# Seven block products instead of eight for one token group's MLP up projection, and a new order of the two groups

## The chip, the core and the metric

The kernel runs on one core of a Trainium2 chip. The metric is device time in microseconds (us) of one launch, as the median of several runs. A core has five engines that run side by side and wait for each other through semaphores: TensorE (PE in the profile; PEld is its weight load), VectorE (DVE), ScalarE (ACT), GpSimd (POOL) and SyncE (SP), which here issues most of the transfers. Matmuls write PSUM, eight banks of 128 x 512 floats; everything else lives in SBUF.

## The reference

The program is one layer of a hybrid decoder over 1024 prompt tokens and 64 sampled tokens (8 sequences of 8), with a model width of 1024. The part that the change touches is the end of the layer:

```python
x = x + mixed @ lw['w_out']
h2 = rmsnorm(x, lw['g_mlp'])
x = x + jnp.square(jax.nn.relu(h2 @ lw['w_up'])) @ lw['w_down']
gate = jax.nn.sigmoid(rmsnorm(x, lw['g_ple']) @ lw['w_ple_gate'])
x = x + gate * (p @ lw['w_ple_proj'])
```

w_up is 1024 x 4096, w_down 4096 x 1024; all data are 32-bit floats. Ahead of this stand the input projection, the three mixers (a recurrent one, a short convolution, and attention, for the sampled tokens over a paged cache) that produce `mixed`.

## The kernel before

**Precision.** A float operand is split in two parts of the type fp32r: a rounded high part (ScalarE copies it to that type) and the remainder (VectorE or GpSimd subtracts). A product of two split operands is three matmuls, high x high, high x low, low x high, accumulated in PSUM (`gemm_t`, L162). Weights are loaded in 512 KB pieces into a raw buffer "wr" (two of them), ScalarE casts them and GpSimd, or VectorE for w_down, subtracts (`Weights.load`, L147). The split weights have two buffers for each part.

**Token groups.** The 1088 tokens are held transposed (model dimension on partitions). Group A is tokens 0 to 511, in one chunk of 512 columns; group B is the other 576 (512 prompt and 64 sampled) in two chunks of 288. `Part` (L1157) holds a group's residual x, its operands h (tag "big"), its activations (tag "act", four buffers) and scratch (tag "tmp").

**The MLP.** It goes in 16 blocks of 256 columns of w_up. `up(parts, fb)` (L1252) multiplies a block's weights with h, and takes max(., 0) times the norm's factor rb, squares it (rb is a token's 1/rms, so h itself doesn't wait for it), and splits the result into ah and al. `down(parts, fb, acts)` (L1269) multiplies these with the matching rows of w_down and adds the result to x, 128 rows and one chunk at a time. `mlp` (L1283) issues the up of block n+1 ahead of the down of block n. PSUM results of both go round three banks (`acc`).

**Order.** The code is written in an order of priority. A scheduler at build time plays it through and lets each engine take the first instruction that is ready, so work written later fills gaps ahead of it; the order on each engine is then fixed. Buffers of a pool go round, and a new pool placed over a released one waits for the tiles that it covers. Group A's output projection, norm and first 14 blocks are written behind attention and decode, and fill TensorE there. `out_proj(B)` can only start when decode is done. The calls in question:

```python
    out_proj(A, 4, 4)
    A.norm("g_mlp", acc, wide=True)
    mlp(*(([A], fb) for fb in range(NA - 1)))
    out_proj(B)
    B.norm("g_mlp", banks(6, 7))
    mlp(([A], NA - 1), *(([B], fb) for fb in range(NA)), *(([A, B], fb) for fb in range(NA, 16)))
```

With NA = 15, block 14 of A follows B's output projection, then come B's blocks 0 to 14, and block 15 for both groups together, whose weights are loaded once. Last come the norms for both groups (`Part.norm`, L1199), the gate and the output (`ple`, L1340). `norm` writes x times the gain, split, as h, and forms rb from the squares: sums on VectorE and GpSimd, a matmul against ones, a root, a reciprocal, and a matmul that spreads it.

Of the kernel before, what the change touches and what calls it, by code (L numbers as in the profile page):

```python
# [41 lines left out]
NA = 15  # L42
# [6 lines left out]
def hybrid_step(ctx: ExitStack, tc: tile.TileContext, I, O):  # L49
# [6 lines left out]
    def f(t):  # L56
        return t.bitcast(F32)
# [958 lines left out]
    W = Weights(wpool)  # L1016
    mpa = tc.alloc_tile_pool(name="mlp_a", bufs=1, reuse_waits="tile")
# [139 lines left out]
    class Part:  # L1157


        def __init__(self, pool, t0, n, chunks):  # L1160
            self.pool, self.t0, self.n, self.chunks = pool, t0, n, chunks
            self.x = pool.tile([128, 8, n], F32, name="x")
            self.tiles = range(t0 // 128, -(-(t0 + n) // 128))

        def big(self, name):
            return [[self.pool.tile([128, 4, self.n], F32R, name=f"{name}{e}{g}", tag="big", bufs=4) for g in range(2)]
                    for e in "hl"]
# [31 lines left out]
        def norm(self, gain, bank, wide=False):  # L1199

            self.h = self.big("n")
            for m in range(8):
                hi, lo = (self.h[e][m // 4][:, m % 4, :] for e in range(2))
                S.activation(hi, self.x[:, m], AF.Copy, scale=P1(gain, m))
                V.scalar_tensor_tensor(lo, self.x[:, m], P1(gain, m), f(hi), op0=ALU.mult, op1=ALU.subtract)  # L1205
            sums, sq = self.act("sums", F32), [self.act("sq", F32) for _ in range(2)]
# [31 lines left out]

    w_up, w_down = I["w_up"][0], I["w_down"][0]

    def out_proj(p, k0=0, nk=8, bank=acc):
        nm = 16 // nk
        x = [h[k0 // 4:] for h in p.h]
        for m0 in range(0, 8, nm):
            w = W.load(w_out[k0 * 128:(k0 + nk) * 128, m0 * 128:(m0 + nm) * 128], nk=nk, ncol=nm * 128)
            for m in range(m0, m0 + nm):
                for t0, n in p.chunks:
                    ps = bank()
                    gemm_t(ps, w, m - m0, x, t0, n, nk=nk)
                    V.tensor_add(p.x[:, m, t0:t0 + n], ps[:, :n], p.x[:, m, t0:t0 + n])  # L1250

    def up(parts, fb):  # L1252
        w = W.load(w_up[:, fb * 256:fb * 256 + 256])
        acts = []
        for p in parts:
            ah, al = p.act("ah", F32R), p.act("al", F32R)
            acts.append((ah, al))
            for m in range(2):
                for t0, n in p.chunks:
                    ps = acc()  # L1260
                    gemm_t(ps, w, m, p.h, t0, n)
                    r = p.tmp("r")
                    V.scalar_tensor_tensor(r[:, :n], ps[:, :n], 0.0, p.rb[:, t0:t0 + n], op0=ALU.max, op1=ALU.mult)  # L1263
                    S.square(r[:, :n], r[:, :n])
                    S.copy(ah[:, m, t0:t0 + n], r[:, :n])
                    V.tensor_sub(al[:, m, t0:t0 + n], r[:, :n], f(ah[:, m, t0:t0 + n]))
        return parts, fb, acts

    def down(parts, fb, acts):  # L1269
        wh, wl = W.load(w_down[fb * 256:fb * 256 + 256, :], nk=2, ncol=1024, sub=V)  # L1270
        for p, (ah, al) in zip(parts, acts):
            for m in range(8):
                c = slice(m * 128, m * 128 + 128)
                for t0, n in p.chunks:
                    ps = acc()
                    for k in range(2):
                        a, b = ah[:, k, t0:t0 + n], al[:, k, t0:t0 + n]
                        PE.matmul(ps[:, :n], wh[:, k, c], a, start=k == 0, stop=False)  # L1278
                        PE.matmul(ps[:, :n], wh[:, k, c], b, start=False, stop=False)  # L1279
                        PE.matmul(ps[:, :n], wl[:, k, c], a, start=False, stop=k == 1)  # L1280
                    V.tensor_add(p.x[:, m, t0:t0 + n], ps[:, :n], p.x[:, m, t0:t0 + n])  # L1281

    def mlp(*blocks):  # L1283

        before = None
        for parts, fb in blocks:
            u = up(parts, fb)
            if before:
                down(*before)
            before = u  # L1290
        down(*before)
# [3 lines left out]
    A = Part(mpa, 0, 512, ((0, 512),))  # L1295
# [15 lines left out]
    B = Part(mpb, 512, 576, ((0, 288), (288, 288)))  # L1311
# [53 lines left out]
    for p in (A, B):  # L1365
        p.norm("g_ple", banks(3, 4))
        ple_inputs(p)
    for sl in range(4):
        w = W.load(wg_[:, sl * 256:sl * 256 + 256])
        w2_ = W.load(wp_[:, sl * 256:sl * 256 + 256], nk=2, tag="wp")  # L1370
# [4 lines left out]
    mpa.release()  # L1375
# [28 lines left out]
```

## Time and profile before

| | us |
|---|---|
| median of 3 runs | 1771.43 |
| lowest, highest | 1764.46, 1772.76 |
| the profiled execution, its own time | 1768.19 |
| span in its profile | 1766.5 |
| TensorE busy | 1700.9 (96%) |
| VectorE busy | 1013.9 (57%) |
| ScalarE busy | 702.3 (40%) |
| GpSimd busy | 484.9 (27%) |

The span is from the first to the last instruction of the profiled execution; the 1.7 us beside it lie outside of the span. A matmul's duration in the profile covers its way through the array, and the next one starts earlier, so the number of matmuls in a stretch tells more than their durations. In rows of the timeline the columns are start, duration, engine, line, operation, output and inputs with their shapes; a bracket gives idle time ahead and what ended it. Rows of groups have a count, the busy time and the mean duration in ns.

### The profile page before, as it was taken

How to read it: one execution, taken by the hardware profiler on the slowest of the kernel's cores; microseconds unless marked ns; L12 is line 12 of the kernel's file. 1: busy time of each engine (PE TensorE's matmuls, PEld its weight loads, DVE VectorE, ACT ScalarE, POOL GpSimd, SP SyncE). 2: the span in 40 equal slices, each digit the busy share in tenths (PEclk: the TensorE clock that was granted, in tenths of full speed). 3: DMA queues.
4: the chain of work that ended last, by engine and by line, in shares of the span. 5: the costliest groups of instructions: out<-in, count | busy, mean ns of one | idle time of the engine just before them, and what ended most of it. 6: DMA issues, size and time to landing. Idle time of an engine off the chain costs nothing.

```text
span 1766.5 us, 29840 instructions
## 1 busy us (share of the span) xinstructions
PE 1700.9 (96%) x11933; PEld 1522.0 (86%) x11933; DVE 1013.9 (57%) x1634; ACT 702.3 (40%) x1283; POOL 484.9 (27%) x412
## 2 busy tenths in 40 slices
PE   6999899999999899999998999999999999999998
PEld 5898888888988777888876666999999999998898
DVE  6266954554576689778754334345555555548432
ACT  6633323323453567555533332442232223235321
POOL 4123322312300353232335452332221221113310
PEclk9999999999999899999999999999999999999999
DMA  5134356434523553333245453532222222221221
GB/s 183 50 115 136 106 151 178 117 92 118 139 77 110 188 173 95 128 124 112 85 122 166 140 161 106 176 94 90 79 76 92 76 92 72 96 75 53 67 63 40
DMA packets 195149, 194.87 MB, mean 110 GB/s; under 512 B 57729, under 2 KB 166945, under 8 KB 194882
## 3 DMA queue, kind: packets, MB, share of 16 engines
q1 hardware_dynamic: 189890, 176.18, 33.3%
q0 software_dynamic: 5120, 16.78, 3.2%
q8 instruction: 94, 1.54, 0.4%
q14 instruction: 45, 0.37, 0.1%
HBM read 155.92 MB, written 36.98 MB: 109 GB/s over the span
## 4 chain that ended last, share of the span: by engine, by line
PE 56%; DVE 3%; DMA 2%; POOL 1%; issue 1%; ACT 0%; SPq 0%; ACTq 0%; POOLq 0%; DVEq 0%
PE b L170 10%; PE b L171 10%; PE b L169 10%; PE b L1278 6%; PE b L1279 6%; PE b L1280 6%; PE b L910 1%; DVE nl L1205 1%; PE b L1145 1%; PE b L1120 1%; PE b L1115 1%; DMA kpg<-in_cache_k,idx 1%; PE b L921 1%; PE b L920 1%; DVE x L1281 1%
## 5 line engine op out<-in xcount | busy, mean ns | idle before, releaser
L159 POOL TENSOR_TENSOR wl<-wr,wh 128x1024 fp32r<-128x1024 f32 (+1 forms) x116 | 291.6, 2532 | 580.8 <-ACT wh L158 571.0
L169 PE MATMUL b<-nh,wh 128*128 128x288 f32 (+1 forms) x960 | 316.1, 330 | 2.2 <-DVE x L1250 2.2
L170 PE MATMUL b<-nl,wh 128*128 128x288 f32 (+1 forms) x960 | 315.9, 329 | 1.6 <-DVE nl L1205 1.6
L171 PE MATMUL b<-nh,wl 128*128 128x288 f32 (+1 forms) x960 | 315.2, 329 | 0.0
L158 ACT CAST wh<-wr 128x1024 fp32r<-128x1024 f32 (+1 forms) x178 | 177.7, 1041 | 277.9 <-PE b L1279 183.5
L1281 DVE TENSOR_TENSOR x<-b,x 128x288 f32<-128x288 f32 (+1 forms) x384 | 200.7, 532 | 130.9 <-PE b L1280 130.7
L1278 PE MATMUL b<-ah,wh 128*128 128x288 f32 (+1 forms) x768 | 256.9, 334 | 6.5 <-DVE x L1281 6.0
L1280 PE MATMUL b<-ah,wl 128*128 128x288 f32 (+1 forms) x768 | 251.9, 328 | 0.0
L1279 PE MATMUL b<-al,wh 128*128 128x288 f32 (+1 forms) x768 | 251.9, 328 | 0.0
L170 PEld LDWEIGHTS b<-nl,wh 128*128 128x128 f32 x960 | 180.5, 188 | 16.1 <-issue 2.7
L169 PEld LDWEIGHTS b<-nh,wh 128*128 128x128 f32 x960 | 180.3, 188 | 16.3 <-DVE x L1250 2.9
L171 PEld LDWEIGHTS b<-nh,wl 128*128 128x128 f32 x960 | 180.4, 188 | 12.7 <-issue 0.8
L1278 PEld LDWEIGHTS b<-ah,wh 128*128 128x128 f32 x768 | 144.6, 188 | 25.4 <-DVE x L1281 9.9
L1279 PEld LDWEIGHTS b<-al,wh 128*128 128x128 f32 x768 | 144.7, 188 | 10.4 <-issue 1.6
L1280 PEld LDWEIGHTS b<-ah,wl 128*128 128x128 f32 x768 | 144.5, 188 | 10.2
L790 PE MATMUL b<-wh,h_hi 128*128 128x256 f32 x432 | 129.4, 300 | 3.7 <-ACT nat L797 3.7
L791 PE MATMUL b<-wl,h_hi 128*128 128x256 f32 x432 | 127.1, 294 | 0.0
L792 PE MATMUL b<-wh,h_lo 128*128 128x256 f32 x432 | 127.0, 294 | 0.0
L1263 DVE SCALAR_TENSOR_TENSOR r<-b,rb 128x288 f32<-128x288 f32 (+1 forms) x96 | 51.0, 533 | 119.7 <-PE b L171 116.8
L169 PE MATMUL b<-h_hi,wh 128*128 128x384 f32 (+1 forms) x336 | 115.5, 344 | 1.4 <-ACT xs L330 1.3
L170 PE MATMUL b<-h_lo,wh 128*128 128x384 f32 (+1 forms) x336 | 113.4, 337 | 0.0
L171 PE MATMUL b<-h_hi,wl 128*128 128x384 f32 (+1 forms) x336 | 112.5, 335 | 0.0
(375 smaller groups left out, 3286.5 us busy)
## 6 DMA issues: line engine op xcount, KB each, us to landing
wr<-in_w_up SPq DMA_DIRECT2D x62, 512.0 KB
wr<-in_w_down SPq DMA_DIRECT2D x62, 512.0 KB
wr<-in_w_in SPq DMA_DIRECT2D x26, 512.0 KB
wr<-in_w_out SPq DMA_DIRECT2D x16, 512.0 KB
xt<-in_x_prompt SPq DMA_DIRECT2D x8, 512.0 KB
stk_s<-sth SPq DMA_DIRECT2D x32, 128.0 KB
stk_s<-stl SPq DMA_DIRECT2D x32, 128.0 KB
out<-nat SPq DMA_DIRECT2D x16, 256.0 KB
```

The source lines that it names most:

```text
L158: S.copy(wh[:, flat], raw[:, :n * ncol])
L159: (sub or G).tensor_sub(wl[:, flat], raw[:, :n * ncol], f(wh[:, flat]))
L169: PE.matmul(ps[:, :n], wh[:, k, c], a, start=(k == 0), stop=False)
L170: PE.matmul(ps[:, :n], wh[:, k, c], b, start=False, stop=False)
L171: PE.matmul(ps[:, :n], wl[:, k, c], a, start=False, stop=(k == nk - 1))
L790: PE.matmul(o, a, w[0][:, k, :], start=(k == 0), stop=False)
L791: PE.matmul(o, a, w[1][:, k, :], start=False, stop=False)
L792: PE.matmul(o, b, w[0][:, k, :], start=False, stop=(k == 7))
L1278: PE.matmul(ps[:, :n], wh[:, k, c], a, start=k == 0, stop=False)
L1279: PE.matmul(ps[:, :n], wh[:, k, c], b, start=False, stop=False)
L1280: PE.matmul(ps[:, :n], wl[:, k, c], a, start=False, stop=k == 1)
L1281: V.tensor_add(p.x[:, m, t0:t0 + n], ps[:, :n], p.x[:, m, t0:t0 + n])
```

## The change

**Seven products.** For group B, the up product of a block is seen as a 2 x 2 block product: the weights in four blocks a[m, k] (128 columns m, half k of the 1024 inputs), h in four blocks (half of the inputs, chunk of 288 tokens). Winograd's form of Strassen's scheme forms it from seven products of block sums instead of eight products of blocks. `up7` makes four sums of weight blocks on GpSimd (`s_`), splits seven weight operands (three into the common ring "w", four into buffers "ws"), runs seven products of four k each, and combines them with seven additions on VectorE, p1 being copied by ScalarE. `operands` makes B's seven split operands from x, the gain and rb: the sums are of normalized values, so rb has to be there first, and the evacuation no longer multiplies by it. The differences run on VectorE, the remainders on GpSimd for 11, 2, 3, 4 and on VectorE for 21, 1, 22. The products go round banks 0 to 3, the downs of B banks 4 to 7.

**Order.** A's block 14 up moves ahead of `out_proj(B)`; behind it come B's `rms` (the second half of `norm`) and its operands 11, 2, 3, 4, then A's up 15 and downs 14 and 15. Then A's h and work pools are released, B's operands 21, 1, 22 and the buffers of `up7` are placed over them, and B's 16 blocks run alone. A's norm for the gate is written ahead of B's last down.

**Weights in pieces.** `load` cuts a load into pieces of 128 x 512, high and low, in a ring of ten each, in place of whole loads in two buffers; the raw loads are the same 512 KB. All products read them through `gemm_p`. Block 15's weights are loaded for A and for B.

```diff
+    def split_piece(src, sub=None, pool=None, tag="w", bufs=10):
+        hl = [(pool or wpool).tile([128, 512], F32R, name=f"{tag}{e}", bufs=bufs) for e in "hl"]
+        h3, l3 = (t.rearrange("p (k c) -> p k c", k=src.shape[1]) for t in hl)
+        S.copy(h3, src)
+        (sub or G).tensor_sub(l3, src, f(h3))
+        return hl
...
+        def operands(self, gain, ids, pool, bufs):
...
+            for k in range(4):
+                h = self.act("hk", F32)
+                for e in range(2):
+                    V.scalar_tensor_tensor(h[:, e], self.x[:, 4 * e + k], P1(gain, 4 * e + k), self.rb, op0=ALU.mult,
+                                           op1=ALU.mult)
+                t = self.act("tk", F32)
+                val = {11: h[:, 0, :n], 21: h[:, 1, :n], 22: h[:, 1, n:], 1: t[:, 0, :n], 2: t[:, 0, n:],
+                       3: t[:, 1, :n], 4: t[:, 1, n:]}
+                if need & {1, 2, 4}:
+                    V.tensor_sub(val[1], h[:, 0, n:], val[11])
+                if need & {2, 4}:
+                    V.tensor_sub(val[2], val[22], val[1])
+                if 4 in need:
+                    V.tensor_sub(val[4], val[21], val[2])
+                if 3 in need:
+                    V.tensor_sub(val[3], val[22], h[:, 0, n:])
+                for i in ids:
+                    S.copy(out[i][:, 0, k], val[i])
+                    (V if i in (21, 1, 22) else G).tensor_sub(out[i][:, 1, k], val[i], f(out[i][:, 0, k]))
...
+    def up7(p, fb, ops, pool):
+        r = [raw_weights(w_up, 4 * k, 4, fb * 256, 256) for k in range(2)]
+        a = {(m, k): r[k][:, :, 128 * m:128 * m + 128] for m in range(2) for k in range(2)}
...
+        w = {11: split_piece(a[0, 0])}
+        G.tensor_add(s_[0], a[1, 0], a[1, 1])
+        G.tensor_sub(s_[1], s_[0], a[0, 0])
+        G.tensor_sub(s_[2], a[0, 0], a[1, 0])
+        w[12] = split_piece(a[0, 1])
+        G.tensor_sub(s_[3], a[0, 1], s_[1])
+        w[22] = split_piece(a[1, 1])
+        for i in (2, 1, 3, 4):
+            w[i] = split_piece(s_[i - 1], pool=pool, tag="ws", bufs=4)
...
+        def out(m, e, c):
+            t = slice(e * n, e * n + n)
+            V.scalar_tensor_tensor(c, c, 0.0, c, op0=ALU.max, op1=ALU.mult)
+            S.copy(ah[:, m, t], c)
+            G.tensor_sub(al[:, m, t], c, f(ah[:, m, t]))
...
+        p1 = pool.tile([128, n], F32, name="p1")
+        S.copy(p1, product(11, 11))
+        out(0, 0, add("c", product(12, 21), p1))
+        u2 = add("u2", product(2, 2), p1)
+        p5 = product(1, 1)
+        v = add("v", p5, u2)
+        u3 = add("u3", product(3, 3), u2)
+        out(1, 1, add("c", p5, u3))
+        out(0, 1, add("c", product(4, 22), v))
+        out(1, 0, add("c", product(22, 4), u3))
...
-    mlp(*(([A], fb) for fb in range(NA - 1)))
+    u = up(A, 0)
+    for fb in range(1, NA):
+        u, before = up(A, fb), u
+        down(*before)
     out_proj(B)
-    B.norm("g_mlp", banks(6, 7))
-    mlp(([A], NA - 1), *(([B], fb) for fb in range(NA)), *(([A, B], fb) for fb in range(NA, 16)))
+    B.rms(banks(6, 7))
+    ops = B.operands("g_mlp", (11, 2, 3, 4), mpb, 4)
+    for fb in range(NA, 16):
+        u, before = up(A, fb), u
+        if fb < 15:
+            down(*before)
+    down(*before)
+    down(*u)
+    wka.release()
+    hpa.release()
+    hpb = tc.alloc_tile_pool(name="h_b", bufs=1, reuse_waits="tile")
+    ops.update(B.operands("g_mlp", (21, 1, 22), hpb, 3))
+    up_bank, down_bank = banks(0, 1, 2, 3), banks(4, 5, 6, 7)
+    u = up7(B, 0, ops, hpb)
+    for fb in range(1, 16):
+        u, before = up7(B, fb, ops, hpb), u
+        down(*before, bank=down_bank)
...
-    for p in (A, B):
-        p.norm("g_ple", banks(3, 4))
-        ple_inputs(p)
+    A.norm("g_ple", banks(0, 1))
+    ple_inputs(A)
+    down(*u, bank=down_bank)
+    B.norm("g_ple", banks(3, 4))
+    ple_inputs(B)
```

More of the change, by code (lines that the diff above doesn't have):

```diff
@@ L1237, in norm @@
                     V.reciprocal(self.rb[:, t0:t0 + n], self.rb[:, t0:t0 + n])
+        def operands(self, gain, ids, pool, bufs):
+            n = self.n // 2
+            out = {}
+            for i in ids:
+                t = pool.tile([128, 4, 2 * n], F32R, name=f"op{i}", tag="big", bufs=bufs)
+                out[i] = t.rearrange("p k t -> p (k t)").rearrange("p (e k t) -> p e k t", e=2, k=4)
+            need = set(ids)
+            for k in range(4):
[14 more added lines that the diff above has]
+                    V.tensor_sub(val[3], val[22], h[:, 0, n:])
+                for i in ids:
+                    S.copy(out[i][:, 0, k], val[i])
+                    (V if i in (21, 1, 22) else G).tensor_sub(out[i][:, 1, k], val[i], f(out[i][:, 0, k]))
+            return out
     w_up, w_down = I["w_up"][0], I["w_down"][0]
@@ L1248, in out_proj @@
                     ps = bank()
-                    gemm_t(ps, w, m - m0, x, t0, n, nk=nk)
+                    gemm_p(ps, w, m - m0, x, t0, n, nk=nk)
                     V.tensor_add(p.x[:, m, t0:t0 + n], ps[:, :n], p.x[:, m, t0:t0 + n])
[L1252 to L1291, printed above, removed]
+    def up(p, fb):
+        w = load(w_up[:, fb * 256:fb * 256 + 256], 8, 256)
+        ah, al = p.act("ah", F32R), p.act("al", F32R)
+        for m in range(2):
+            for t0, n in p.chunks:
+                ps = acc()
+                gemm_p(ps, w, m, p.h, t0, n)
+                r = p.tmp("r")
+                V.scalar_tensor_tensor(r[:, :n], ps[:, :n], 0.0, p.rb[:, t0:t0 + n], op0=ALU.max, op1=ALU.mult)
+                S.square(r[:, :n], r[:, :n])
+                S.copy(ah[:, m, t0:t0 + n], r[:, :n])
+                V.tensor_sub(al[:, m, t0:t0 + n], r[:, :n], f(ah[:, m, t0:t0 + n]))
+        return p, fb, ah, al
@@ L1293, in hybrid_step, with down @@
+    def down(p, fb, ah, al, bank=acc):
+        w = load(w_down[fb * 256:fb * 256 + 256, :], 2, 1024, sub=V)
+        for m in range(8):
+            for t0, n in p.chunks:
+                ps = bank()
+                gemm_p(ps, w, m, ([ah], [al]), t0, n, nk=2)
+                V.tensor_add(p.x[:, m, t0:t0 + n], ps[:, :n], p.x[:, m, t0:t0 + n])
     w_out = I["w_out"][0]
-    A = Part(mpa, 0, 512, ((0, 512),))
+    A = Part(xpa, wka, hpa, 0, 512, ((0, 512),))
     A.load_x(acc)
@@ L1310, in hybrid_step @@
     mpb = tc.alloc_tile_pool(name="mlp_b", bufs=1, side="right", reuse_waits="tile")
-    B = Part(mpb, 512, 576, ((0, 288), (288, 288)))
+    B = Part(mpb, mpb, mpb, 512, 576, ((0, 288), (288, 288)))
     B.load_mix(range(8))
@@ L1374, in hybrid_step @@
     mpb.release()
-    mpa.release()
+    wka.release()
+    xpa.release()
     wpool.release()
```

75 lines of the change are left out of this document (64 added, 11 removed).

## The prediction, made before the change was run

> **What bounds the kernel now.** I read the page's engine totals and its forty slices first, then busy time by stage, then the groups of one steady stretch.
>
> ```profile
> span 1766.5 us, 29840 instructions
> PE 1700.9 (96%) x11933; PEld 1522.0 (86%) x11933; DVE 1013.9 (57%) x1634; ACT 702.3 (40%) x1283; POOL 484.9 (27%) x412
> PE   6999899999999899999998999999999999999998
> ```
>
> ```profile
> core 0: us, PE busy (x) PEld busy (x) DVE busy (x) ACT busy (x) POOL busy (x), PEclk, DMA share, GB/s
> 900.00:950.00 50.00, 43.18 (x247) 31.58 (x245) 23.41 (x45) 15.19 (x25) 30.29 (x27) 0.93 0.55 160
> ...
> 1300.00:1350.00 50.00, 50.00 (x379) 50.00 (x379) 26.48 (x52) 14.83 (x24) 9.04 (x5) 1.00 0.26 79
> ...
> 1600.00:1650.00 50.00, 46.16 (x272) 39.79 (x271) 40.85 (x61) 31.24 (x55) 23.40 (x12) 1.00 0.18 55
> ...
> 1700.00:1766.00 66.00, 61.10 (x388) 55.95 (x386) 19.42 (x37) 12.25 (x27) 3.67 (x2) 0.99 0.15 43
> ```
>
> TensorE is the bound: in 1300:1350 it has no gap, while VectorE (DVE) is busy 26.5 of 50 us, GpSimd (POOL) 9.0, and the DMA share is 0.26. So removing a matmul there removes time, as long as nothing else rises to 50. A matmul's listed duration isn't its price, since matmuls overlap: 379 in 50 us is **0.132 us each** at 288 columns. For 512 columns I count starts:
>
> ```profile
> 900.58 0.39 PE L171 MATMUL b<-nh,wl 128*128 128x512 f32 x1
> ...
> 903.30 0.39 PE L171 MATMUL b<-nh,wl 128*128 128x512 f32 x1
> ```
>
> Twelve matmuls in 2.72 us: **0.227 us each**. The steady groups between 1250 and 1550 us give the other prices (count, busy us, mean ns):
>
> ```profile
> L171 PE MATMUL b<-nh,wl 128*128 128x288 f32 x384 | 113.2, 295 | 0.0
> L1281 DVE TENSOR_TENSOR x<-b,x 128x288 f32<-128x288 f32 x186 | 84.0, 456 | 54.9 <-PE b L1280 54.9
> L159 POOL TENSOR_TENSOR wl<-wr,wh 128x1024 fp32r<-128x1024 f32 x23 | 57.3, 2513 | 245.7 <-ACT wh L158 245.7
> L158 ACT CAST wh<-wr 128x1024 fp32r<-128x1024 f32 x48 | 48.1, 1049 | 139.3 <-PE b L1279 118.7 <-PE b L170 20.5
> L159 DVE TENSOR_TENSOR wl<-wr,wh 128x1024 fp32r<-128x1024 f32 x24 | 28.3, 1222 | 5.9 <-ACT wh L158 5.9
> L1266 DVE TENSOR_TENSOR al<-r,ah 128x288 fp32r<-128x288 f32 x47 | 27.6, 587 | 35.2 <-ACT ah L1265 35.2
> L1265 ACT CAST ah<-r 128x288 fp32r<-128x288 f32 x47 | 20.4, 434 | 1.5
> ```
>
> **Part 1, the matmuls removed.** A block is 256 columns of w_up and the matching rows of w_down. For B a block's up product is now 2 row tiles x 2 token chunks x 8 k x 3 terms = 96 matmuls of 288 columns; seven products x 4 k x 3 terms are 84 of the same shape. Sixteen blocks: 192 fewer, x 0.132 = **-25.3 us**. A steady B block (up and down) falls from 192 matmuls, 25.3 us, to 180, 23.7 us.
>
> **Part 2, what the seven products ask of the other engines, per 23.7 us block.** GpSimd: seven weight splits and four sums or differences of 512 columns at half of 2.513 (1.26 us), four activation remainders of 288 columns at 0.72 (half of the 1.43 us quoted below for 576): 13.8 + 2.9 = 16.7 us, up from about 5. VectorE: 16 output adds and 7 product adds at 0.456, four squarings at 0.415, four splits of w_down at 0.61: 14.6 us. ScalarE: 11 casts at 0.52 and five copies at 0.434: 7.9 us. All lie beside 23.7 us of TensorE. The loads stay 2 MB a block; A's last block is no longer shared, so four 512 KB loads on SP's queue and their splits are added, at a DMA share of 0.26: 0 us, and some 5 us in all if the next weights were late, which the ring of ten pieces, seven a block, makes unlikely. If cover is thin it is at VectorE: an operation with two SBUF inputs can meet a GpSimd operation.
>
> ```profile
> 1599.95 4.78 POOL L159 TENSOR_TENSOR wl<-wr,wh 128x1024 fp32r<-128x1024 f32 x2 [45.06 <-ACT wh L158]
> ...
> 1602.33 2.95 DVE L1205 SCALAR_TENSOR_TENSOR nl<-x,par,nh 128x512 fp32r<-128x512 f32 x1
> ...
> 1605.80 0.74 DVE L1205 SCALAR_TENSOR_TENSOR nl<-x,par,nh 128x512 fp32r<-128x512 f32 x1
> ...
> PE b L1278 <- DVE x L1281: 3.3, 7, 1.5
> ...
> L1205 DVE SCALAR_TENSOR_TENSOR nl<-x,par,nh 128x576 fp32r<-128x576 f32 x16 | 15.7, 1005 | 2.4 <-ACT nh L1204 2.4
> ```
>
> The same instruction took 0.74 us with GpSimd idle and 2.95 us when GpSimd was in its second subtraction (1602.3 to 1604.7); operations whose other input is PSUM (456 ns throughout) show nothing of it. Eight of VectorE's 31 operations per new block are of the first kind; each may wait up to 1.26 us, and TensorE's evacuations queue behind it. Two runs of four PSUM banks allow about three groups (3 x 6 x 0.132 = 2.4 us) of delay. From the waits row, seven such stalls cost 3.3 us in the one stretch where VectorE was as mixed; I take 0.2 us a block, **+3 us**, ends 0 and 16 (1 us a block).
>
> The page "SBUF — State Buffer" of the Trainium skill, section "Who interferes with whom", says that a VectorE instruction with two SBUF inputs and a GpSimd instruction that reads SBUF exclude each other for a whole instruction. By that rule, the trace agrees (2.95 against 0.74 us).
>
> **Part 3, the gap before B's first new product.** This is the term I had to choose. B's operands can be formed only from the finished x and its norm, and B's first block needs all of op11 and op21. What covers this is A's block 15 up, and downs 14 and 15: 3 x 48 matmuls x 0.227 = 32.7 us after out_proj(B). Before, only rb was late, and it was needed only at an evacuation.
>
> ```profile
> 1167.99 0.29 PE L171 MATMUL b<-mh,wl 128*128 128x288 f32 x1
> 1168.12 0.39 PE L169 MATMUL b<-nh,wh 128*128 128x512 f32 x1
> ...
> 1168.86 0.45 DVE L1250 TENSOR_TENSOR x<-b,x 128x288 f32<-128x288 f32 x1
> 1169.23 3.73 DVE L1205 SCALAR_TENSOR_TENSOR nl<-x,par,nh 128x576 fp32r<-128x576 f32 x5
> ...
> 1180.21 1.17 PE L1220 MATMUL b<-onesq,sums 128*128 128x1 f32 x10
> ...
> 1187.46 0.70 ACT L1231 COPY rb<-b 128x512 f32<-128x512 f32 x2 [2.47 <-PE b L1229]
> ...
> 1189.73 0.83 DVE L1266 TENSOR_TENSOR al<-r,ah 128x288 fp32r<-128x288 f32 x2 [0.83 <-ACT ah L1265]
> ...
> 1195.56 0.69 DVE L1281 TENSOR_TENSOR x<-b,x 128x512 f32<-128x512 f32 x1 [0.91 <-PE b L1280]
> ...
> 1150.62 1.43 POOL L1211 TENSOR_TENSOR sums<-sums,sq 128x576 f32<-128x576 f32 x1 [1.43 <-ACT sq L1209]
> ```
>
> Let 0 be the end of out_proj(B) on TensorE (1168.1). The last x is there at 1.2, its square and two sums take 2.2 more, and from the sums' matmuls to rb were 7.9 us (1180.21 to 1188.1): rb at 11; 7 if no queue delays it. Then VectorE forms operands 11, 2, 3, 4: eight products of 576 columns at 0.746 (3.73 for five) and 16 differences of 288 at 0.415 (0.83 for two), 12.6 us; then 21, 1, 22: eight products, four differences and 12 remainders, 12.6 us again. They take the same "act" buffers, so the second set follows the first. Between them VectorE must serve A: 16 adds and four evacuation steps of 512 columns at 0.69 and eight w_down splits at 0.61, 18.7 us, of which I put 14 after rb. op21 is complete at 11 + 25.2 + 14 = 50. TensorE's cover with its first product (12 x 0.132) ends at 34.2: **+15.8 us** idle; and behind that product wait all of B's later products and downs. Low end: rb at 7 and only the 11 us of adds, 43, idle 9. High end: GpSimd's remainders for 11, 2, 3, 4 (16 x 0.72 = 11.5 us) and part of the first block's weights (14 us) exclude VectorE: 65, idle 31. I take the middle, nearer the low end, because adds from PSUM can run under GpSimd and the group above was stretched by a third (1005 against 746 ns), not doubled.
>
> After such a gap TensorE restarts at a lower clock: 900:950 shows a granted clock of 0.93 beside 6.8 us of idle time, 3.5 us of full clock in 50. I take **+2 us**, ends 0 and 3.5.
>
> The page "TensorE: Matmul & The Clock Gate" of the Trainium skill, section "What's actually happening", puts the clock at half after an idle window of about 3.4 us and back after as long a busy one: an estimate of 1.7 us for one gap; the 0.93 above agrees that gaps lower it.
>
> **Part 4, the ends.** At the end 3.8 + 4.9 us are idle (46.16 of 50, 61.10 of 66). A's last norm and its p loads on SP may now run under B's downs 14 and 15 instead of 15 alone, with four banks instead of three: **-1 us**, ends -4 and +3. Up to 1100 us the same A blocks fill decode and attention, with one up (10.9 us) more to fill with; weights come in finer pieces: 0, ends -3 and +3.
>
> **Sum**, against the profiled execution's 1768.2 us: -25.3 + 15.8 + 2 + 3 - 1 = -5.5, 1762.7. The median of the runs shown is 3.2 us above that execution (1771.4), so I forecast **1766**. The measurement can tell about 0.5%, 8.9 us, from no change.
>
> **The rivals.**
> *The gap is covered (faster).* rb comes at 7, GpSimd's remainders hide, the gap is 5 us with little clock loss: -25.3 + 5 + 1 + 2 - 1 = -18, 1753. For it: the 50 us of VectorE work is a queue sum, and the schedule may put A's splits before rb. Against it: the 25.2 us of operands alone end at 36. Chance 0.3.
> *VectorE and GpSimd exclude each other through both operand sets (slower).* Place: from rb to op21. Gap 31, clock 3.5, steady stalls 5, end -1: +13, 1785. It decides from a gap of 28 us on, where these costs exceed the saving by 0.5%. For it: the 2.95 us row. Against: the mean of 1005. Chance 0.17. By the rule of the page "SBUF — State Buffer" of the Trainium skill, which excludes whole instructions, this would be the case.
> *GpSimd becomes the bound of the B blocks (slower).* Its 15 operations need 23.7 us, so 1.6 us on average instead of 1.1. For it: under contention such operations were longer:
>
> ```profile
> L159 POOL TENSOR_TENSOR wl<-wr,wh 128x512 fp32r<-128x512 f32 x4 | 6.2, 1545 | 3.3 <-ACT wh L158 3.3
> L1211 POOL TENSOR_TENSOR sums<-sums,sq 128x512 f32<-128x512 f32 x6 | 10.3, 1710 | 7.7 <-ACT sq L1209 7.6
> ```
>
> At 1.71 and 0.97 a block takes 22.7 us, still under; at 25.3 the saving is gone and 1788 is left. Chance 0.08.
>
> **How the numbers follow.** Forecast 0.45, rivals 0.3, 0.17, 0.08. The forecast's own range is -12 to +2 (1759 to 1773); a quarter of it is beyond -8.9. Faster 0.3 + 0.1 = 0.40; slower 0.25 less the rivals' mild parts, 0.23; same 0.37. The range takes in the covered case and most of the exclusive one: 1750 to 1785.
>
> **What would show it.** TensorE's count 192 lower, and 180 matmuls per 23.7 us in steady B blocks (379 in 50 us) with no idle time; POOL at 17 to 21 us of 23.7. One gap after A's last down, on TensorE, ended by VectorE or ScalarE at the first products; its length decides. VectorE operations on two SBUF inputs stretched beyond 0.75 us while GpSimd runs. I am wrong in mechanism if the gap is under 5 us, if TensorE waits inside the steady blocks for weights, or if idle time appears in 900:1100.

## The result, and the profile after

The changed kernel takes **1780.49 us** (median of 20 runs, 1773.96 to 1784.28), the kernel before on the same chip 1771.49 (20 runs): a ratio of 1.0052, 95% interval 1.0039 to 1.0065. It is 0.5% slower, where 1766, 0.3% faster, was forecast; it lies inside the stated range of 1750 to 1785, on the other side of no change. Every ratio below is against the kernel before on the chip of that run; a few disturbed executions are left out of the ratios. The profiled execution is 10.1 us longer than the one of before (1776.6 against 1766.5 us).

The page of the changed kernel, its first lines and TensorE's forty slices:

```profile
span 1776.6 us, 30204 instructions
PE 1687.8 (95%) x11741; PEld 1504.5 (85%) x11741; DVE 1097.3 (62%) x1788; ACT 743.7 (42%) x1459; POOL 746.1 (42%) x694
PE   6999899999999899999989999996989999999998
```

TensorE runs 192 matmuls fewer (11933 to 11741), as the change says. Slices 28 and 30 (1199 to 1244 and 1288 to 1332 us) now are a 6 and an 8, where before stood nines. Busy time by stage shows the place and its size:

```profile
core 0: us, PE busy (x) PEld busy (x) DVE busy (x) ACT busy (x) POOL busy (x), PEclk, DMA share, GB/s
1177.00:1200.00 23.00, 21.29 (x106) 17.69 (x105) 15.17 (x24) 10.46 (x19) 5.76 (x6) 1.00 0.17 47
1200.00:1250.00 50.00, 33.63 (x163) 27.87 (x162) 47.57 (x61) 16.09 (x38) 37.52 (x30) 0.86 0.11 32
1250.00:1300.00 50.00, 45.49 (x337) 44.56 (x335) 39.18 (x62) 20.29 (x41) 46.56 (x38) 1.00 0.34 98
1300.00:1350.00 50.00, 47.20 (x339) 46.35 (x338) 35.70 (x62) 16.96 (x33) 41.45 (x33) 0.97 0.32 95
1350.00:1400.00 50.00, 50.00 (x378) 50.00 (x377) 35.23 (x64) 17.18 (x33) 39.32 (x32) 1.00 0.31 94
```

From 1350 on a stretch holds 378 matmuls and no idle time, as 1300:1350 did before (379): there nothing stands in the way of the saving, 192 x 0.132 = 25.3 us. Ahead of 1350, in 1200:1250, TensorE is busy for 33.6 of 50 us at a granted clock of 0.86 while VectorE has hardly a free moment (47.57 of 50). Now the account. out_proj(B) ends on TensorE at 1177.25, where it ended at 1168.12:

```profile
1177.25 0.39 PE L1062 MATMUL b<-nh,wh 128*128 128x512 f32 x1
...
1218.30 0.39 PE L1064 MATMUL b<-ah,wl 128*128 128x512 f32 x1
1220.74 0.37 PE L1369 MATMUL b<-op,wh 128*128 128x288 f32 x1 [2.05 <-DVE x L1406]
...
1226.00 0.61 PE L1370 MATMUL b<-op,wh 128*128 128x288 f32 x1 [3.30 <-DVE op L1317]
...
1238.98 0.61 PE L1370 MATMUL b<-op,wsh 128*128 128x288 f32 x1 [5.16 <-DVE op L1317]
```

One more A up (10.9 us) lies ahead of that point, so the part up to it got 1.8 us shorter. Behind it TensorE had 144 matmuls of A at 0.227 and, up to 1250, 99 of B's new products at 0.132: 45.8 us of work in 72.75, **27 us lost**, where the kernel before lost 2.3 us in as long a stretch (the norm's small matmuls are in both): 24.7 us come with the change. In 1250 to 1350 it ran 676 where 100 us hold 757: **10.8 us lost**. The end didn't get shorter: from 1600 on the kernel before has 140.0 us of matmuls (282 of 512 columns, 576 of 288) in 166.5, the changed one 148.3 us (240 and 711) in 176.6, so it has 1.8 us more beside them. Then -25.3 + 24.7 + 10.8 - 1.8 + 1.8 is +10.2 us, against 10.1 measured.

The idle time isn't one gap but waits, most of 1 to 5 us. All of them, from 1177 to 1250, end with VectorE: 11.0 us with remainders of the second operand set (L1317), 6.9 us with its adds for A (L1406), which stand in the same queue.

```profile
PE b L1370 <- DVE op L1317: 11.0, 4, 5.2
PE b L1062 <- DVE x L1406: 4.8, 4, 2.0
PE b L1369 <- DVE x L1406: 2.1, 1, 2.1
```

The groups of VectorE's work from rb to the last remainder, 1192 to 1246 us:

```profile
L1302 DVE SCALAR_TENSOR_TENSOR hk<-x,par,rb 128x576 f32<-128x576 f32 x16 | 17.7, 1142 | 0.2 <-ACT rb L1282 0.2
L1406 DVE TENSOR_TENSOR x<-b,x 128x512 f32<-128x512 f32 x15 | 10.1, 678 | 0.0
L1317 DVE TENSOR_TENSOR op<-hk,op 128x288 fp32r<-128x288 f32 x8 | 8.1, 1043 | 0.0
L1308 DVE TENSOR_TENSOR tk<-hk 128x288 f32<-128x288 f32 x8 | 6.8, 852 | 0.0
L1317 DVE TENSOR_TENSOR op<-tk,op 128x288 fp32r<-128x288 f32 x4 | 3.9, 986 | 0.0
L1314 DVE TENSOR_TENSOR tk<-hk 128x288 f32<-128x288 f32 x4 | 3.3, 832 | 0.0
L1310 DVE TENSOR_TENSOR tk<-hk,tk 128x288 f32<-128x288 f32 x4 | 3.3, 829 | 0.0
L1312 DVE TENSOR_TENSOR tk<-hk,tk 128x288 f32<-128x288 f32 x4 | 2.9, 716 | 0.0
```

All of it but the adds (L1406) makes operands: 48 operations (16 products, 20 differences, 12 remainders; where an expectation below counts 44, and 28 subtractions, it is 48 and 32), **46.0 us**, where the prediction had 25.2. VectorE has no idle time from its first product to its last remainder. The adds, with one input in PSUM, kept 0.68 us. Single rows of VectorE's timeline, and one of GpSimd's beside them:

```profile
1224.42 0.68 DVE L1406 TENSOR_TENSOR x<-b,x 128x512 f32<-128x512 f32 x1
...
1226.24 2.96 DVE L1317 TENSOR_TENSOR op<-hk,op 128x288 fp32r<-128x288 f32 x2
...
1244.67 0.45 DVE L1317 TENSOR_TENSOR op<-tk,op 128x288 fp32r<-128x288 f32 x1
```

```profile
1225.90 4.43 POOL L1043 TENSOR_TENSOR wsl<-s,wsh 128x512 fp32r<-128x512 f32 x3 [0.27 <-ACT wsh L1042]
```

Two remainders of 0.45 us took 2.96 us while GpSimd made three remainders of weights, by then those of B's first block. The last operand was there at 1245.1, **67.9 us** behind out_proj(B)'s end.

### The profile page after: what moved, and what is told of

Its sections match the earlier page's. It is cut to its first block, busy times and chain, and to the rows that moved or that the text cites. A ratio compares the mean times of both kernels' runs of the same rounds, so it can differ in the third digit from the quotient of the medians.

```text
span 1776.6 us, 30204 instructions
## 1 busy us (share of the span) xinstructions
PE 1687.8 (95%) x11741; PEld 1504.5 (85%) x11741; DVE 1097.3 (62%) x1788; ACT 743.7 (42%) x1459; POOL 746.1 (42%) x694
## 4 chain that ended last, share of the span: by engine, by line
PE 72%; DVE 12%; DMA 5%; issue 4%; ACT 3%; POOL 2%; SPq 2%; ACTq 0%; DVEq 0%; POOLq 0%
PE b L1062 12%; PE b L1064 12%; PE b L1063 12%; PE b L1369 3%; PE b L169 3%; PE b L1371 3%; PE b L1370 3%; PE b L170 3%; PE b L171 2%; PE b L790 2%; PE b L791 1%; PE b L792 1%; PE b L910 1%; DVE x L1406 1%; PE b L1192 1%
## 5 line engine op out<-in xcount | busy, mean ns | idle before, releaser
L1043 POOL TENSOR_TENSOR wl<-wr,wh 128x512 fp32r<-128x512 f32 x164 | 226.9, 1389 | 239.4 <-ACT wh L1042 220.0
L1042 ACT CAST wh<-wr 128x512 fp32r<-128x512 f32 x292 | 179.0, 623 | 342.7 <-PE b L1063 200.0
L1406 DVE TENSOR_TENSOR x<-b,x 128x288 f32<-128x288 f32 (+1 forms) x384 | 195.8, 528 | 95.4 <-PE b L1064 94.2
L1062 PE MATMUL b<-nh,wh 128*128 128x512 f32 (+1 forms) x448 | 166.3, 372 | 2.5 <-DVE x L1331 1.6
L1063 PE MATMUL b<-nl,wh 128*128 128x512 f32 (+1 forms) x448 | 165.9, 370 | 0.0
L1064 PE MATMUL b<-nh,wl 128*128 128x512 f32 (+1 forms) x448 | 164.8, 368 | 0.0
L1064 PEld LDWEIGHTS b<-ah,wl 128*128 128x128 f32 x768 | 144.9, 189 | 10.3
L1043 DVE TENSOR_TENSOR wl<-wr,wh 128x512 fp32r<-128x512 f32 x128 | 110.7, 869 | 50.2 <-ACT wh L1042 46.2
L890 DVE TENSOR_TENSOR_SCAN keep<-keep,onesq 128x128 f32<-128x128 f32 (+3 forms) x64 | 93.3, 1463 | 33.7 <-ACT keep L889 33.2
L159 POOL TENSOR_TENSOR wl<-wr,wh 128x1024 fp32r<-128x1024 f32 x26 | 68.8, 2656 | 94.1 <-ACT wh L158 94.1
L1062 PEld LDWEIGHTS b<-nh,wh 128*128 128x128 f32 x448 | 84.7, 189 | 18.8 <-DVE x L1406 2.6
```

Source lines behind the costliest of these rows:

```text
L1042: S.copy(h3, src)
L1043: (sub or G).tensor_sub(l3, src, f(h3))
L1062: PE.matmul(ps[:, :n], w(0, k, m), a, start=(k == 0), stop=False)
L1063: PE.matmul(ps[:, :n], w(0, k, m), b, start=False, stop=False)
L1064: PE.matmul(ps[:, :n], w(1, k, m), a, start=False, stop=(k == nk - 1))
```

## The experiments

The letters in the expectations: X, VectorE's and GpSimd's operations on SBUF hold each other up while operands are made; Q, VectorE's queue is simply full; W, the weights of the first blocks come late; C, too little of A's work covers the operands; S, the second set waits for the end of A's work. "Last remainder" is counted from out_proj(B)'s end on TensorE, and is 67.9 us in the changed kernel. Times, not single profiled spans, decide: out_proj(B) ended anywhere from 1174 to 1185 us in the profiled executions with NA = 15, and the profiled executions of two kernels below (the weights of the first two blocks; rb left out) were the slowest of all of theirs.

### The new order without the seven products

```diff
-    B.rms(banks(6, 7))
-    ops = B.operands("g_mlp", (11, 2, 3, 4), mpb, 4)
+    B.norm("g_mlp", banks(6, 7))
...
-        u, before = up7(B, fb, ops, hpb), u
+        u, before = up(B, fb), u
```

> The new order of the groups and the weights in pieces alone: B's blocks with eight products (ordinary up and norm), 192 matmuls more than the changed kernel. If the loss comes from forming B's operands and from the load on GpSimd (theories X, Q and W below alike), it goes with them: the span from the end of B's output projection on has no gap over 4 us, and the time is that of the kernel before, 1768 (1764 to 1773). If instead the order or the pieces cost, the time is above 1780, up to 1780 + 25 = 1805.

1769.81 us, ratio 1.0013 (0.9999 to 1.0027). TensorE has no idle time from 1150 to 1600 us:

```profile
1150.00:1250.00 100.00, 100.00 (x656) 94.30 (x656) 61.23 (x98) 47.52 (x85) 30.07 (x21) 1.00 0.31 92
1250.00:1350.00 100.00, 100.00 (x757) 100.00 (x756) 53.92 (x110) 33.52 (x64) 20.78 (x16) 1.00 0.27 83
```

The order, the pieces and block 15's second load cost about nothing. All that is lost comes with the seven products.

### Work taken from one engine or the other

Remainders of the first set on VectorE:

```diff
-                    (V if i in (21, 1, 22) else G).tensor_sub(out[i][:, 1, k], val[i], f(out[i][:, 0, k]))
+                    V.tensor_sub(out[i][:, 1, k], val[i], f(out[i][:, 0, k]))
```

> The 16 remainders of operands 11, 2, 3, 4 on VectorE instead of GpSimd. Theory X (VectorE and GpSimd hold each other up over operations with two SBUF inputs): 16 GpSimd operations of 0.99 us leave, 16 of 0.415 come: op21 is complete 5 to 9 us earlier, time 1772 to 1776. Theory W (B's first blocks wait for their weights behind GpSimd and the two raw buffers): GpSimd is free 16 us earlier, the stalls of 1250 to 1350 shrink too, 1768 to 1774. Theory Q (VectorE's own queue sets the gap): 6.6 us more on VectorE, 1785 to 1788.

1783.74 us, 1.0079 (1.0052 to 1.0107), last remainder 70.7 us. X and W, which had the time fall, missed; Q comes nearest. With 16 operations more the last remainder came later, not earlier, as it must where VectorE's queue is full (the two intervals of the time overlap). GpSimd now stood idle for 22.7 us up to 1225.4, and then made weights of blocks 0 and 1 without a break through the second set, which stayed stretched.

Less work for GpSimd: the first set's remainders and the sums and remainders of the weights of B's block 0 are left out, and ScalarE copies in their place.

```diff
+        if quiet:
+            S.copy(l3, src)
...
+                    else:
+                        S.copy(out[i][:, 1, k], val[i])
```

> Left out: the remainders of operands 11, 2, 3, 4, and for B's first block the sums and remainders of the weights; ScalarE writes copies in their place, so GpSimd does nothing from the end of A's weights to B's second block. X: operations of VectorE go back to 0.75 and 0.42 us, op21 is complete at about 50 us after B's output projection instead of 67, time 1757 to 1765. W: the second block's weights start some 25 us earlier, stalls of 1250 to 1350 gone as well, 1753 to 1760. Q: nothing changes on VectorE, 1778 to 1782.

1768.03 us, 0.9998 (0.9983 to 1.0013), last remainder 60.0 us. Against the changed kernel that is 0.54%, some 9.6 us: a quarter of the 37.8 us lost, less than X had. The second set was still stretched, since GpSimd had moved on to the weights of block 1.

The same for the weights of the first two blocks, with the first set's remainders back on GpSimd:

> Left out: the sums and the remainders of the weights in B's first two blocks (ScalarE writes copies instead), so that GpSimd is silent while operands 21, 1, 22 are formed; the remainders of the other operands stay on GpSimd. X (GpSimd's weight work holds VectorE up in the second operand set): the second set takes 13 us instead of 23, the last operand comes 58 us after B's output projection instead of 68, time 1764 to 1769. Q (VectorE's queue alone): last operand at 66 to 68, 1774 to 1778.

1769.05 us, 0.9979 (0.9959 to 1.0000), last remainder 60.0 us. In the second set remainders took 0.45 us again, and the first set's differences stayed stretched, so the operand work came to 32.0 us. Some of the gain was lost again: VectorE now waited 5.8 us for casts of ScalarE, which had the copies to make.

Less work for VectorE: rb is left out of the second set's products, and ScalarE makes them.

```diff
+                    if 21 in need:
+                        S.activation(h[:, e], self.x[:, 4 * e + k], AF.Copy, scale=P1(gain, 4 * e + k))
```

> Left out: the factor rb in operands 21, 1, 22, whose eight products of 576 columns ScalarE makes instead of VectorE. If VectorE's operand chain is what TensorE waits for, the last operand comes earlier by 6 us (their plain time) to 14 us (their stretched time in the changed kernel): 1764 to 1771. If the weights of B's first blocks (GpSimd and the raw buffers) are as late, under 3 us: 1774 to 1778.

1772.27 us, 1.0003 (0.9987 to 1.0019), last remainder 57.9 us. The last operand came 10 us earlier. So far each edit that takes a part of the work away brings back a quarter to a third of the 37.8 us (8.7 to 12.9 by the ratios).

### Weights earlier

```diff
-        raw = wpool.tile([128, 1024], F32, name="wr", bufs=2)
+        raw = wpool.tile([128, 1024], F32, name="wr", bufs=3)
...
-    def split_piece(src, sub=None, pool=None, tag="w", bufs=10):
+    def split_piece(src, sub=None, pool=None, tag="w", bufs=9):
```

> Three raw buffers instead of two (and nine pieces in the ring instead of ten, for the room). W: w_down's raw loads no longer wait for GpSimd to finish with w_up's, the 10.8 us lost in 1250 to 1350 shrink to under 4: 1772 to 1775. X and Q: the gap before 1250 stays, 1778 to 1783.

1778.49 us, 1.0067 (1.0047 to 1.0087). In the profile the idle time of 1250:1350 falls from 7.3 to 1.5 us, so W is right for that place; the time of the runs did not follow (the profiled execution, 1769.74 us, is the fastest of the four by 8.7 us), and the last remainder stood at 69.4 us.

### More cover, another place, another order

out_proj(B) one block of A earlier, and two:

```diff
-NA = 15
+NA = 14
```

> One A block more behind B's output projection (NA = 14): 21.8 us more of matmuls between it and B's first product, and 21.8 us fewer to fill TensorE while decode runs. Theory C (the loss is a chain of 67 us from B's output projection to B's last operand, with only 32.7 us of A's matmuls beside it): the gap shrinks by about 20 us, and A's matmuls still last until decode ends, 1758 to 1764. Rival (TensorE is short of work while decode runs, or the lost time is in the blocks' own weights): 1774 to 1782.

1794.02 us, 1.0130 (1.0098 to 1.0162). C had 1758 to 1764 and its rival 1774 to 1782: neither holds. It lost twice. out_proj(B) came before its own input was ready, and TensorE waited 6.2 us for it: 43.84 of 50 us busy in 1100:1150 at a clock of 0.90. And the second set came only at 87.3 us. VectorE's timeline:

```profile
1238.96 0.69 DVE L1406 TENSOR_TENSOR x<-b,x 128x512 f32<-128x512 f32 x1 [0.67 <-PE b L1064]
1239.57 0.45 DVE L1317 TENSOR_TENSOR op<-hk,op 128x288 fp32r<-128x288 f32 x1
```

Between A's adds VectorE waits for TensorE, with the second set's remainders standing behind the adds in its order. The added cover never reached the second set.

> Two A blocks more behind B's output projection (NA = 13): cover of 76 us against a chain of 67. C: no gap at B's first products, but TensorE short of work at the end of decode by 10 to 25 us (idle time in 1060 to 1110): 1760 to 1770. Rival (the gap doesn't depend on the cover): 1774 to 1785.

NA = 13: the four times scatter from 1795.7 to 2959 us, so no ratio is given, but none is below those of NA = 14; in the profile (1794.0 us) the last remainder stands as far behind A's last add as with 14, 16.7 us.

All seven operands beside A's work. The products read the high halves twice, and the remainders go to scratch that nothing reads:

```diff
     ops = B.operands("g_mlp", (11, 2, 3, 4), mpb, 4)
+    ops.update(B.operands("g_mlp", (21, 1, 22), mpb, 4))
...
-    ops.update(B.operands("g_mlp", (21, 1, 22), hpb, 3))
```

> Left out: the products read the high half of an operand twice, and all remainders of B's operands, computed in full as before, go to a small scratch tile that nothing reads; so all seven operands fit beside A's work, and the second set no longer needs the memory that A's blocks use nor stands behind A's last adds on VectorE. VectorE, GpSimd and ScalarE do the same instructions, TensorE as many. Theory S (the second set is late because VectorE reaches it only behind A's last add): the last remainder moves from 68 us behind out_proj(B)'s end to 55 or less, TensorE's idle time in the 70 us from that end falls from 18 to under 8 us, and the time is 0.5 to 0.8% below the changed kernel's, about 0.997 to 1.000 of the kernel before. Theory Q (VectorE has no free time from the sums to the last remainder, so its order doesn't matter): the last remainder stays within 5 us of 68, A's adds come later instead, and the time stays at 1.003 to 1.007 of the kernel before.

1775.88 us, 1.0030 (1.0013 to 1.0047), last remainder 77.0 us, beyond what either theory had. The schedule still put the second set behind A's adds (its first remainder at 1239.2, after the last add at 1227.6), and TensorE doesn't wait for remainders that nothing reads, so alone it tells little. With NA = 14 the schedule did mix them:

> As e10_place, and out_proj(B) one block of A earlier (NA = 14), so that 21.8 us more of A's products lie behind it. With NA = 14 alone the second set came 86 us behind out_proj(B)'s end, right behind A's last add, and VectorE waited for TensorE between A's adds. Theory S: here the second set is ready by 65 us behind out_proj(B)'s end, before A's last product, and there is no idle time between A's last product and B's block 0 that an operand ends (sum of waits on op and hk under 3 us); what NA = 14 loses in front of out_proj(B), about 12 us, stays, so the time is 1.000 to 1.005 of the kernel before, against 1.013. Theory Q: the operands' making is stretched along with the cover, the second set comes at 80 us or later, and the time stays over 1.008.

1784.90 us, 1.0093 (1.0060 to 1.0126), last remainder 80.3 us. That is Q's outcome, and S falls. The second set's remainders now begin at 1218.6, ahead of A's last add at 1250.6, and operands and adds are slow together:

```profile
1200.00:1210.00 10.00, 9.57 (x43) 7.59 (x41) 10.00 (x14) 4.26 (x9) 5.92 (x5) 1.00 0.27 70
1210.00:1220.00 10.00, 2.88 (x7) 2.30 (x8) 10.00 (x10) 4.58 (x10) 9.14 (x9) 0.60 0.11 38
1220.00:1230.00 10.00, 7.39 (x27) 5.21 (x25) 10.00 (x12) 2.99 (x7) 8.73 (x6) 0.89 0.34 105
```

VectorE is busy without a break, GpSimd for 9 of 10 us, and TensorE stops in the middle of A's own blocks. Operands aren't a delay that cover hides: the cover needs VectorE as well.

The products that need only the first set written first, and three raw buffers:

```diff
         S.copy(p1, product(11, 11))
-        out(0, 0, add("c", product(12, 21), p1))
         u2 = add("u2", product(2, 2), p1)
+        u3 = add("u3", product(3, 3), u2)
+        out(1, 0, add("c", product(22, 4), u3))
+        out(0, 0, add("c", product(12, 21), p1))
         p5 = product(1, 1)
...
-        u3 = add("u3", product(3, 3), u2)
...
-        out(1, 0, add("c", product(22, 4), u3))
```

> The changed kernel with three raw weight buffers and a ring of nine pieces, and the seven products emitted with the four that need only the first operand set ahead (11, 2, 3, 22 by operand 4), then the three of the second set. If the order of the products is part of the gap: three more products, 4.7 us, run before the first wait for the second set, the idle time from out_proj(B)'s end on falls by 3 to 5 us beside the 6 us that the raw buffers save in 1250 to 1350, and the time is 1770 to 1774 where the kernel before has 1770 (0.999 to 1.003). If the compiler's order had already run these products where it could (in the changed kernel parts of products 2 and 3 stood before the last waits): no change against the three buffers alone, 1.004 to 1.007.

1781.49 us, 1.0058 (1.0037 to 1.0080): no gain. In the changed kernel, too, products 2 and 3 ran before the last remainders were there (weights "wsh" from 1229.9 on), and 1230:1240 here has 3.13 us of TensorE work in 10.

### The pair itself

Both halves of GpSimd's work in the stretch left out: the first set's remainders, and the weights' sums and remainders in B's first two blocks (the edits of the two kernels above, together).

> Left out: the remainders of the first operand set and the sums and remainders of the weights of B's first two blocks; ScalarE copies something of the same size in their place, so that GpSimd has next to nothing to do from the end of B's out projection until B's third block. All work of VectorE and TensorE stays. Theory X (GpSimd's two-source work stretches VectorE's two-source work and that is what makes the operands late): the 44 operand operations on VectorE, 46.0 us in the changed kernel, take 25 us or less (products about 0.76, subtractions about 0.45), the last remainder comes 52 us or less behind the end of out_proj(B), and the time is 0.991 to 0.996 of the kernel before, some 1% below the changed kernel. Rival (ScalarE's casts, or the order of VectorE's queue, hold the operands): the operations get short but VectorE waits between them, the last remainder stays at 58 us or later, and the time is 0.997 to 1.000, as with each half of the left-out work alone.

**1760.20 us, 0.9942** (0.9921 to 0.9963). VectorE's groups, 1194 to 1233 us:

```profile
L1305 DVE SCALAR_TENSOR_TENSOR hk<-x,par,rb 128x576 f32<-128x576 f32 x16 | 12.4, 819 | 0.2
L1420 DVE TENSOR_TENSOR x<-b,x 128x512 f32<-128x512 f32 x15 | 10.3, 691 | 0.0
L1311 DVE TENSOR_TENSOR tk<-hk 128x288 f32<-128x288 f32 x8 | 3.7, 458 | 0.0
L1321 DVE TENSOR_TENSOR op<-hk,op 128x288 fp32r<-128x288 f32 x8 | 3.4, 456 | 2.5 <-ACT op L1319 2.5
L1315 DVE TENSOR_TENSOR tk<-hk,tk 128x288 f32<-128x288 f32 x4 | 1.8, 456 | 0.0
...
L1321 DVE TENSOR_TENSOR op<-tk,op 128x288 fp32r<-128x288 f32 x4 | 1.8, 456 | 0.5 <-ACT op L1319 0.5
```

The same 48 operations take 26.7 us for 46.0, every group of subtractions 0.456 to 0.458 us on average (two groups of four stand between the shown ones), and the adds what they took before. ScalarE, which now makes copies too, isn't what stretched them; VectorE only waits 3.0 us for its casts. The last remainder comes at 52.8 us. The bounds given, 25 and 52 us, were missed by a little; the time lies where X put it. Counted as above, TensorE loses 9.5 us in the 72.75 us behind out_proj(B), where the changed kernel lost 27, and some 8 us in the next 100, where it lost 11.

From the other side, with all of GpSimd's work in place: rb stays in two PSUM banks, so a product has one input in SBUF.

```diff
-                    V.scalar_tensor_tensor(h[:, e], self.x[:, 4 * e + k], P1(gain, 4 * e + k), self.rb, op0=ALU.mult,
-                                           op1=ALU.mult)
+                    for j in range(2):
+                        V.scalar_tensor_tensor(h[:, e, n * j:n * j + n], self.x[:, 4 * e + k, n * j:n * j + n],
+                                               P1(gain, 4 * e + k), self.rb[j][:, :n], op0=ALU.mult, op1=ALU.mult)
```

> The inverse roots stay in two PSUM banks, and the 16 products of 576 columns become 32 of 288 with one source in PSUM; nothing is left out. Theory X: an operation with one source in PSUM isn't stretched (A's adds kept 0.68 us among the stretched ones), so the products take 32 x 0.46 = 14.7 us where the changed kernel had 17.7, all near one duration; the 28 subtractions stay stretched (28.3 us); the last remainder comes 2 to 5 us earlier, and the time is 1.002 to 1.005 of the kernel before. If VectorE is stretched by anything else (any source in SBUF): the products' durations scatter up to twice the shortest and there is no gain, 1.005 to 1.008.

1775.03 us, 1.0029 (1.0012 to 1.0046), last remainder 62.1 us.

```profile
L1315 DVE SCALAR_TENSOR_TENSOR hk<-x,par,b 128x288 f32<-128x288 f32 x32 | 14.4, 502 | 0.0
...
L1321 DVE TENSOR_TENSOR tk<-hk 128x288 f32<-128x288 f32 x8 | 7.9, 982 | 0.0
L1330 DVE TENSOR_TENSOR op<-hk,op 128x288 fp32r<-128x288 f32 x8 | 7.5, 963 | 0.0
```

The products lost their stretch although each is now two instructions; most of the subtractions, two inputs in SBUF, kept theirs (26.1 us for 28.3). This is the mechanism without anything left out. Of the 5.8 us by which the last remainder comes earlier, 1.0 is rb itself, which ScalarE no longer copies. For the time the gain isn't shown: the interval overlaps the changed kernel's.

> As e12_rb_psum, with three raw weight buffers and a ring of nine pieces. With three buffers alone the profile lost its waits of 1250 to 1350 but the times didn't move. If the two gains add: 0.998 to 1.003. If the raw buffers only move the waits: as e12_rb_psum, within 0.002.

With three raw buffers on top: 1771.84 us, 1.0012 (0.9986 to 1.0037), the best of the kernels with seven products that do all the work, level with the kernel before. Idle time in 1250:1350 is 0.24 us, against 4.05 and 2.79 in its halves with two raw buffers.

```profile
1250.00:1300.00 50.00, 49.76 (x373) 49.30 (x372) 38.38 (x67) 18.93 (x37) 50.00 (x40) 1.00 0.29 96
1300.00:1350.00 50.00, 50.00 (x378) 49.99 (x377) 38.20 (x66) 18.20 (x34) 42.71 (x35) 1.00 0.32 96
```

The intervals of the times with two and with three raw buffers overlap, so what the third buffer is worth in time stays open.

| | operand work on VectorE, us | last remainder, us | lost in 72.75 us behind out_proj(B), us | ratio |
|---|---|---|---|---|
| GpSimd's work of both kinds left out | 26.7 | 52.8 | 9.5 | 0.9942 |
| weights' work of two blocks left out | 32.0 | 60.0 | 18.7 | 0.9979 |
| remainders and block 0's weights left out | 35.7 | 60.0 | 20.6 | 0.9998 |
| rb in PSUM | 40.5 | 62.1 | 24.0 | 1.0029 |
| changed kernel | 46.0 | 67.9 | 27.0 | 1.0052 |

From the last row to the first, 19.3 us less of operand work go with 1.1% of the time, 19.5 us, of which 17.5 lie in the stretch where the operands are formed and every wait of the changed kernel ended with VectorE. Some 3 us more lie in the 100 us behind it, where the weights were late. The first three columns are of one profiled execution each, the ratio is of all.

## Why the prediction was wrong, point by point

**Part 1 was right.** 192 fewer matmuls, 378 in 50 us: -25.3 us.

**Part 2 was right in the steady blocks and wrong in the first ones.** VectorE is busy for 35.2 of 50 us (16.7 of a 23.7 us block, for 14.6 worked out), GpSimd for 19 (16.7), ScalarE for 8.0 (7.9), and no stall is left there: the +3 us were too many. But "the next weights were late", put at 0, happened in 1250:1350, for 10.8 us. The longest of these waits:

```profile
1289.70 1.29 POOL L1355 TENSOR_TENSOR s<-s,wr 128x512 f32<-128x512 f32 x1
1291.02 3.15 SPq L1036 DMA_DIRECT2D wr<-in_w_down  x2
1295.51 2.51 DVE L1043 TENSOR_TENSOR wl<-wr,wh 128x512 fp32r<-128x512 f32 x2 [4.18 <-ACT wh L1042]
```

A w_down load leaves as GpSimd ends its last read of a raw buffer with w_up; VectorE waits 4.2 us for the cast of what it brings, and TensorE 2.7 us for VectorE's next add. The ring of ten pieces, named as the protection, didn't help a load that waits for a raw buffer. With three raw buffers such waits were rarer in each of the three profiles (idle time 1.5, 0.24 and, in the kernel with the products reordered, 7.0 us, of which operands make up 3.5). GpSimd was not the bound of the steady blocks; in 1250:1300 it was busy for 46.6 of 50 us, and here its pace set when the loads left.

**Part 3 failed, at "I take the middle, nearer the low end".** The row that it chose by, 1005 ns for 746, was read as a stretch by a third. It is a mean of two kinds. Twelve of its 16 operations had no GpSimd operation beside them and took 0.80 to 0.82 us, and one that met GpSimd in its last part took 0.81; the three that ran into GpSimd's work took 1.45, 1.59 and 2.48. Two of these, with GpSimd's rows, in the kernel before:

```profile
1172.39 5.71 POOL L159 TENSOR_TENSOR wl<-wr,wh 128x1024 fp32r<-128x1024 f32 x2 [7.62 <-ACT wh L158]
1174.39 1.45 DVE L1205 SCALAR_TENSOR_TENSOR nl<-x,par,nh 128x576 fp32r<-128x576 f32 x1
...
1635.88 5.26 POOL L159 TENSOR_TENSOR wl<-wr,wh 128x1024 fp32r<-128x1024 f32 x2
1636.41 2.48 DVE L1205 SCALAR_TENSOR_TENSOR nl<-x,par,nh 128x576 fp32r<-128x576 f32 x1 [0.57 <-ACT nh L1204]
```

So operations beside GpSimd took about twice their time there too, and in the changed kernel GpSimd is busy for 37.5 of 50 us. The terms and what they measured: rb 11, measured 15.2 (the sums were ready at 3.1, but their matmuls stand behind A's in TensorE's order and began at 7.5); the operands 25.2, measured 46.0; service to A behind rb 14, measured 10.1 (all of it adds; the splits of w_down fell elsewhere). Neighbours overlap by some 0.08 us in these durations, so rb and VectorE's work end at 67.9 us, beyond the high end of 65. That end held the remainders (11.5 us, measured 15.9) and a part of block 0's weights; block 1's weights, which GpSimd began at 1233.9 behind them, were in no term. With GpSimd silent the last operand came at 52.8, near the sum of 50 at plain durations, in part by luck: rb was 4 us later and the service to A 4 us shorter.

TensorE lost 24.7 us there, clock included, where 15.8 and 2 were put: 6.9 us more. The weights and stalls cost 10.8 us for 3, 7.8 more, and the ends 0 for -1. That makes 15.7 us, from the -5.5 forecast to +10.2. With either of the two misses alone the sum would be +1.4 or +2.3. The gap was not larger still, 67.9 less the cover of 34.2, because TensorE ran parts of later products in the pauses, while the prediction had them all wait behind op21.

The rival "VectorE and GpSimd exclude each other through both operand sets" has the mechanism that happened. That its sum (31 + 3.5 + 5 - 1 - 25.3 = +13) is near the 10.1 measured is partly luck: its gap and clock were 34.5 us, measured 24.7, its steady stalls of 5 us didn't occur, and late weights, which it doesn't have, cost 10.8.

By the rule of the page "SBUF — State Buffer" of the Trainium skill, section "Who interferes with whom" (a VectorE instruction with two SBUF inputs contends with a GpSimd instruction that reads SBUF, one with at most one SBUF input doesn't), the trace agrees: subtractions of 0.456 us with GpSimd silent against group means of 0.72 to 1.04, and 0.68 throughout for the adds from PSUM.

**The clock.** Taken as +2, ends 0 and 3.5. The granted clock was 0.86 in 1200:1250, 7 us of full clock in 50. Half of that fell into waits, where it costs nothing: 26 matmuls of 288 columns followed each other in 0.24 to 0.41 us for 0.132, 3.5 us in all, part of the 27 us above.

**Part 4.** The end got 1.8 us longer (-1 worked out), the part ahead of out_proj(B)'s end 1.8 us shorter (0).

## What to carry to other kernels

Before an operation moves onto VectorE or GpSimd, count for the stretch where it lands how long both read SBUF: beside a busy GpSimd, VectorE's two-input work cost 1.7 times its plain price here (46.0 against 26.7 us), and a longer cover didn't help, since the cover needs VectorE too. Don't read that price from the mean of a group: look at which of its operations met the other engine. Keep one input of such work in PSUM where a bank is free (17.7 to 14.4 us here, with twice as many instructions). An algorithm that saves matmuls pays in sums and remainders; here the saving went where those don't run beside TensorE, at the first blocks.

## What the runs showed that was not expected

The pair is not even: in the changed kernel GpSimd's 16 remainders of 288 columns took 0.99 us on average, the shortest 0.80, while VectorE's 32 subtractions went from 0.456 to 0.88. And the length of a stall alone doesn't tell whether TensorE restarts slowly: behind a wait of 2.71 us (at 1298) matmuls followed each other in 0.13 us, behind one of 2.24 us (at 1320) soon in 0.24. The granted clock fell at 1225.7, 1236.0 and 1321.3 us, 10.3 and 85.3 us apart, 3 and 25 steps of 3.41. Cut into such steps, the trace shows it halve behind one in which TensorE was busy for little:

```profile
1218.90:1222.30 3.40, 1.56 (x12) 1.59 (x13) 3.40 (x5) 1.53 (x4) 3.40 (x4) 1.00 0.00 0
1222.30:1225.70 3.40, 0.40 (x4) 0.16 (x2) 3.40 (x4) 1.56 (x4) 3.25 (x2) 1.00 0.16 25
1225.70:1229.10 3.40, 1.09 (x3) 0.74 (x3) 3.40 (x4) 1.16 (x3) 3.20 (x3) 0.51 0.85 257
...
1317.90:1321.30 3.40, 1.16 (x9) 0.89 (x7) 3.40 (x7) 0.71 (x2) 2.77 (x3) 1.00 0.55 154
1321.30:1324.70 3.40, 3.40 (x16) 3.29 (x15) 2.42 (x7) 1.19 (x3) 2.50 (x2) 0.50 0.14 25
```

Behind 0.40 and 1.16 us of work in 3.4 the clock is half, behind 1.56 it is full; 1.32 us (1232.5 to 1235.9) is followed by half and 1.83 us (1293.9 to 1297.4) by full. These five steps alone don't make a rule.

The page "TensorE: Matmul & The Clock Gate" of the Trainium skill, section "What's actually happening", has half the clock after an idle window of about 3.4 us and the full one after as long a busy window. The trace agrees on the half, on the length and on the return; but a window that halved the clock here was not idle, it held up to 1.32 us of work.
